# Hybrid decoder layer: later roundings of the mixer's operands, norm rows in the transposes' banks, and the tail of attention merged at its own length

## The chip, the cores and the metric

The kernel runs on one core of one Trainium2 chip. The metric is the device time of one execution in microseconds (us); lower is better. A time given for a kernel is the median of several timed runs. Besides those, one execution is taken with the hardware profiler; it has a time of its own.

## The reference, cut to what matters

A decoder layer with 1024 tokens, width 1024, batch 1, all in float32. A first SwiGLU half, then the mixer, then cross-attention to a fixed memory of 256 tokens, then a second SwiGLU half; each with an RMS norm ahead and behind. The change lies in the mixer and in the keys and values of the memory:

```python
# hybrid_mixer(u): u is the normed stream, 1024 x 1024
proj = u @ w_in
q, k, v, z, xs, bm, cm, dt_raw = jnp.split(proj, ...)
o_att = stick_breaking_attention(heads(q), heads(k), heads(v))   # 16 heads of 64
o_att = rmsnorm(o_att, attn_norm_g)
...
y = ssd_chunked(xs, dt, a, bm, cm) + d_skip[:, None] * xs
y = y.reshape(b_, s_, SSD_WIDTH) * jax.nn.silu(z)
o_ssd = rmsnorm(y in 2 groups of 512, ssd_norm_g)
return jnp.concatenate([o_att, o_ssd], axis=-1) @ w_out          # 2048 -> 1024

# stick_breaking_attention, for a block of queries t and keys s < t
z = q @ k.T / 8
log_a = log_sigmoid(z) + (sum over s < j < t of log_sigmoid(-z[t, j]))
out = exp(log_a) @ v

# memory_cross_attention
k, v = jnp.split(mem_n @ wkv, 2, axis=-1)                         # mem_n: 256 x 1024
```

## The kernel before, in words

**Products.** Every large product is made in float32 precision out of three products of rounded parts: an operand is split into a high part, rounded to the short float format that TensorE takes at full rate, and a low part, the rest. `mm3` (L139) issues high x high, high x low and low x high. A weight tile has 128 output columns and 1024 input rows (8 slices of 128, called k) and is split into `whi` (L261, ScalarE) and `wlo` (L263, VectorE). An activation operand is a tile of 128 channels x 512 tokens; where a norm's gain belongs to it, `scaled_split` makes its high part on ScalarE (L268) and its low part on VectorE (L270). The tokens are worked in two halves of 512, called hh = 0 and 1. A full weight tile with one half is 8 x 3 = 24 products.

**Order of the work.** The program is Python that issues instructions one after the other. For TensorE the order is fixed: each product is tied behind the one issued before it. Beside it runs `self.clock`, the kernel's own count of the cost of the products issued so far (0.422 per column, so 216 for a product with 512 columns, 109 for a transpose). All other engines' instructions are placed by a scheduler, which has a simulation of its own and puts an instruction into its engine's queue where it believes its inputs ready. Three means restrict it: `pinned(at)` holds a piece of work to a point of that clock; a list `self.later` holds pairs of a due time and a function, which is called when the clock has passed the due time, and its instructions are then pinned behind those issued before on their engine; and single instructions pass through `kp`, the same pin. `merge(a, ta, b, tb)` interleaves two generators of work so that they advance in the ratio ta : tb of that clock.

**The stage.** Attention goes through eight pairs of heads. While pair p computes scores, transposes and value products (`units`), the q, k and v projections of pair p + 1 (`inproj`, L1690ff) are merged with it, at 25500 : 32500. With the last pair's projections (p = 7) the function `before(n)` (L1746) is called at 13 steps, n = 0 to 12: seven of them inside the second half of the v projection, six inside the second half of the k projection. It loads the eight SSD operands of the mixer for the first half of the tokens (`XL[0][k]`, L1749, two per step for n = 0 to 3), makes their high and low parts in place (n = 5 to 12, one each), takes the first mixer weight tile (n = 5), and makes the first norm row (n = 10 and 12).

A *norm row* (`rms_rows`, L339) spreads four columns of reciprocal norms, one value per token, over all 128 partitions: four small float32 products (eight instructions in the trace) into a bank of PSUM, here of the tile "ms", then a copy on ScalarE (L349) into `rpre0` or `rpre1`. Two such rows are made for the mixer, one for each of the two SSD groups.

Scores go to PSUM in two buffers `z`, a sigmoid on ScalarE (L1780) writes them to `nb`, and a scan on VectorE (L1784) makes the attention weights in place. These are transposed on TensorE in blocks of four 128 x 128 tiles. The banks for the transposes come from `tr_tile`, a rotation of three: two buffers "tr", then "ms":

```python
turn[0] = (turn[0] + 1) % 3
if turn[0]:
    return self.t(pp, shape, F32, "tr", bufs=2)
return self.t(self.msp, shape, F32, "ms", bufs=1)
```

Each block is then split into `ath` (L261, ScalarE) and `atl` (L263, VectorE), and four value products follow once three blocks are pending. `finish` (L1797 to L1801) evacuates a result and adds it to the mixer's buffer in DRAM (`mix_d`).

**The tail.** After the last projections, `tail()` (L1902) holds the rest of pair 7's attention. `beside()` (L1907) holds the second norm row, six (MIXED) weight tiles of the mixer's SSD half (`mix_first`, L1929, four steps each), and then the values of the memory (`mem_prep`, L1861, loads and splits the memory; `memory_values`, L1872, makes eight products of 24 instructions with 256 columns). The two are merged at 26000 : 52200. `vout` transposes each memory value; the last one is pinned 2500 behind the end of the merge (L1926).

**The mixer behind it.** `mix_out` (L1958) loads the eight attention operands of the first half (`load`, L1978, DMA at L1988, kt = 0 to 7), rounds them (`scaled_split`), and has them squared: `square` (L1968) squares operand 0 into the sum `asum`, and each later one into a tile "sq1", which VectorE then adds to `asum` (L1976). The squares stand in `self.later`, at 500 + 700 kt of the clock behind the loads. The last two tiles of `mix_first` run; then the pass n = 1 takes the eight attention operands, four k of two weight tiles first and then the other four. The norm of the attention output is made from `asum` by small products (`rms_cols`) at 6600 and later. Pass 2 and 3 do the same for the other half of the tokens. The tiles "sq1" and "dg" are shared with the attention: `parts` uses both for the roundings of q and k, `mix_sum` uses "sq1" in the mixer's first tiles, and the last memory value lies in "dg".

Of the kernel before, what the change touches and what calls it, by code (L numbers as in the profile page):

```python
# [10 lines left out]
F32 = mybir.dt.float32  # L11
# [7 lines left out]
P = 128  # L19
S = 1024  # L20
H = 512
# [4 lines left out]
MIXED = 6  # L26
# [21 lines left out]
class Kern:  # L48
# [287 lines left out]
        if r2 is not None:  # L336
            self.kp(nc.vector.tensor_tensor(out=c, in0=c, in1=r2, op=ALU.mult))

    def rms_rows(self, c, r, behind=False):  # L339

        nc = self.nc
        pool, tag = self.msp, "ms"
        nb = c.shape[1]

        def product():
            ps = self.t(pool, [P, H], F32, tag, bufs=1)
            for b in range(nb):
                self.mm(ps[:, b * P : (b + 1) * P], c[:, b : b + 1].to_broadcast([P, P]), self.ident, True, True)
            self.kp(nc.scalar.copy(r, ps[:, 0 : nb * P]))  # L349

        if not behind:
            product()
        return product

# [1256 lines left out]
    def attention(self):  # L1611
        nc, ap = self.nc, self.ap
        with self.pools("at", ["o", "a"], ["w"]) as (op, sp, wsp, pp):
# [52 lines left out]
            def inproj(p):  # L1666
# [12 lines left out]
                def steps(hh, t, before):  # L1679

                    nc.sync.dma_start(out=self.mix_d[p][:, hh * H : (hh + 1) * H], in_=t)
                    dv = self.t(sp, [P, H], F32, "dv", bufs=2)
                    with first():
                        nc.vector.tensor_tensor(out=dv[:, 1:H], in0=t[:, 0 : H - 1], in1=t[:, 1:H], op=ALU.subtract)
                        if before is None:
                            nc.vector.tensor_scalar(out=dv[:, 0:1], in0=t[:, 0:1], scalar1=-1.0, scalar2=None, op0=ALU.mult)
                        else:
                            nc.vector.tensor_tensor(out=dv[:, 0:1], in0=before[:, H - 1 : H], in1=t[:, 0:1], op=ALU.subtract)
                    return dv
# [39 lines left out]
                for n in range(7):  # L1729
                    next(v1)  # L1730
                    if p == 7:
                        before(n)
                    yield
                tv.append(steps(1, evac((yield from v1), 1), t0))
                last = self.proj(wk, 1)
                for n in range(6):
                    next(last)
                    if p == 7:
                        before(7 + n)
                    yield  # L1740
                    if n in (2, 5):
                        vtr(n // 3, tv[n // 3])
                        yield
                kevac(evac((yield from last), 1), h1)

            def before(n):  # L1746

                for k in range(2 * n, 2 * n + 2) if n < 4 else ():
                    nc.sync.dma_start(out=self.XL[0][k].bitcast(F32), in_=self.mix_d[8 + k][:, 0:H])  # L1749
                if n > 4:  # L1750
                    lo = self.XL[0][n - 5]
                    self.scaled_split(self.XH[0][n - 5], lo, lo.bitcast(F32), self.par("ssd_norm_g", n - 5))
                if n == 5:
                    ready.append(next(self.Wo))
                if n == 10:
                    late.append(mix_row(0))
                if n == 12:
                    late.pop()()

            def mix_row(i):  # L1760
                self.mix_r.append(self.t(self.rp, [P, H], F32, f"rpre{i}", bufs=1))
                return self.rms_rows(self.norm_c[i][:, 0:4], self.mix_r[i], True)

            def scores(p, a, c):

# [76 lines left out]
            def drain(n):  # L1842
                while len(prods) > n:
                    prods.pop(0)[1]()
                    yield

            def values(p, a, c, A):
                for jj in range(c + 1):
                    prods.append((p, transpose(p, a, c, A, jj)))
                    yield  # L1850
                    yield from drain(3)

            def units(p):
                for a in range(2):
                    for c in range(4):
                        A = yield from scores(p, a, c)
                        if pend:
                            yield from values(*pend.pop())
                        pend.append((p, a, c, A))

            def mem_prep():  # L1861
                m = [self.t(sp, [P, 4, MEM], F32R, t, bufs=3) for t in ("q", "k", "v")]
                m = [x[:, 2 * i : 2 * i + 2, :] for x in m for i in range(2)]
                m += [x.rearrange("p (a b) -> p a b", a=2) for x in spare]
                for i in range(4):
                    raw = self.t(sp, [P, 2, MEM], F32, "ev", bufs=2)
                    nc.sync.dma_start(out=raw, in_=ap["memT"][:, 2 * i : 2 * i + 2, :])
                    for j in range(2):
                        self.scaled_split(m[i][:, j, :], m[4 + i][:, j, :], raw[:, j, :], self.par("mem_g", 2 * i + j))
                return m[0:4], m[4:8]  # L1870

            def memory_values(mh, ml):  # L1872

                rm = self.t(self.tp, [P, H], F32, "sq1")[:, 0:MEM]
                self.rms_rows(self.mem_c[:, :], rm)
                yield
                for n in range(8):
                    w = ready.pop() if ready else next(Wm)
                    ps = yield from self.kvproj(w, mh, ml)

                    t = self.t(self.tp, [P, H], F32, "dg") if n == 7 else self.t(sp, [P, H], F32, "ev", bufs=2)
                    t = t[:, 0:MEM]
                    with first():
                        nc.vector.tensor_tensor(out=t, in0=ps, in1=rm, op=ALU.mult)
                    pend_v.append((n, t))
                    if n > 0:
                        vout(*pend_v.pop(0))
                        yield
# [13 lines left out]
            def tail():  # L1902
                yield from units(7)
                yield from values(*pend.pop())
                yield from drain(0)

            def beside():  # L1907
                late.append(mix_row(1))
                self.first = self.mix_first(ready.pop())
                for n in range(4 * MIXED):  # L1910
                    if n == 2:
                        late.pop()()
                    if n == 4 * MIXED - 4:
                        ready.append(next(Wm))
                    next(self.first)
                    yield
                yield from memory_values(*mem_prep())
# [3 lines left out]
            self.Wo, self.mix_r, ready, late = self.wstream(wo[0:MIXED]), [], [], []  # L1921
            for p in range(7):
                self.merge(units(p), 25500 if p else 20700, inproj(p + 1), 32500)
            self.merge(tail(), 26000, beside(), 21000 + 5200 * MIXED)
            self.Wo = self.wstream(wo[MIXED:])
            with self.pinned(self.clock + 2500):  # L1926
                vout(*pend_v.pop(0))
# [30 lines left out]
    def mix_out(self):  # L1958
# [3 lines left out]
        with self.pools("mo", ["r", "a"], ["b"]) as (rp, sp, sp2, dnp):  # L1962
# [5 lines left out]
            def square(i, x):  # L1968

                if i == 0:  # L1970
                    asum.append(self.t(sp, [P, H], F32, "asum"))
                    nc.scalar.square(asum[-1], x)
                else:
                    sq = self.t(self.tp, [P, H], F32, "sq1")
                    nc.scalar.square(sq, x)
                    nc.vector.tensor_tensor(out=asum[-1], in0=asum[-1], in1=sq, op=ALU.add)  # L1976

            def load(kt, hh):  # L1978
                if kt < 8:
                    hi = self.t(sp, [P, H], F32R, "ohi", bufs=8)  # L1980
                    lo = self.t(sp, [P, H], F32R, "olo", bufs=8)
                else:
                    hi, lo = self.XH[1][kt % 8], self.t(sp2, [P, H], F32R, "slo", bufs=8)
                    if kt == 8:
                        self.place(sp2, 32)
                raw = self.t(sp, [P, H], F32, "oraw", bufs=8) if kt < 8 else lo.bitcast(F32)
                self.tc.keep_in_program_order(
                    nc.sync.dma_start(out=raw, in_=self.mix_d[kt][:, hh * H : (hh + 1) * H])  # L1988
                )
                if kt < 8:  # L1990
                    self.later.append((self.clock + (500, 3000)[hh] + (700, 1300)[hh] * (kt % (8, 3)[hh]), lambda: square(kt, raw)))
                self.scaled_split(hi, lo, raw, self.par("ssd_norm_g" if kt >= 8 else "attn_norm_g", kt % 8))
                return hi, lo

            passes = [(hh, part) for hh in range(2) for part in (1, 0)]
# [3 lines left out]
            def prefetch(n, k):  # L1999
                if n < 4:  # L2000
                    hh, part = passes[n]
                    acts.setdefault(n, []).append(load(8 * part + k, hh))
# [11 lines left out]
            for n, (hh, part) in enumerate(passes):  # L2014
# [13 lines left out]
                for d0 in range(0, 8, 2):  # L2028
                    ws = [next(W), next(W)]
                    ps = {}  # L2030
# [383 lines left out]
```

## Time and profile before

| what | us |
|---|---|
| median of 3 runs | 2599.42 |
| lowest and highest of these runs | 2598.77 and 2601.72 |
| the profiled execution's own time | 2599.88 |
| span of the profile (first to last instruction) | 2598.1 |
| TensorE busy in the span | 2572.6 (99%) |
| VectorE busy in the span | 1991.7 (77%) |
| ScalarE busy in the span | 1291.8 (50%) |

The profile is one execution, its times count from the start of the span. PE is TensorE's matrix products, PEld its weight loads, DVE is VectorE, ACT is ScalarE, POOL is GpSimd and SP the engine that issues most DMAs. A row of a single instruction gives its start, its duration, engine, line, operation and tiles (out<-in); in brackets stands the idle time of the engine just before it and what ended that idle time. `mm`, `dn`, `z`, `tr`, `ms` are tiles in PSUM; `L139` is the line of the helper that issues all products.

### The profile page before, as it was taken

To read this page: it belongs to the slowest core of one execution; us is meant where nothing else is said; L and a number is where in the kernel's file an instruction comes from. 1 tells how busy PE (TensorE), PEld (TensorE's weight loads), DVE (VectorE), ACT (ScalarE), POOL (GpSimd) and SP (SyncE) were. 2 spreads that over 40 slices of the span, in tenths; PEclk is the share of its full clock that TensorE was granted. 3 is DMA by queue.
4 is the path that set the end of the run, shared out by engine and by line. 5 is a ranking of instruction groups with operands and counts; after the bars stand their busy time and mean duration, and the time that the engine had idled before them with its cause. 6 is when DMAs were issued, how large, how long until landed. Compare 5 with 4: busy or idle time off the path is not lost. (4 is left out here: it accounts for less than half of the span.)

```text
span 2598.1 us, 36782 instructions
## 1 busy us (share of the span) xinstructions
PE 2572.6 (99%) x12850; PEld 2147.1 (83%) x12850; DVE 1991.7 (77%) x3045; ACT 1291.8 (50%) x2300; POOL 576.1 (22%) x668
## 2 busy tenths in 40 slices
PE   9999999999999999999999999999999999999999
PEld 7888888887777788888888898888878888888887
DVE  7889997779689884777777777876656888767767
ACT  7434444555356663555555554445554433333553
POOL 2555553001000001111111110111011755541000
PEclk9999999999999999999999999999999999999999
DMA  6448889655555526555555556647658453327554
GB/s 239 162 174 298 305 293 315 204 186 184 206 209 193 183 70 218 162 154 145 148 155 133 157 171 208 205 162 251 203 182 300 144 176 102 115 80 239 184 175 153
DMA packets 216042, 489.82 MB, mean 189 GB/s; under 512 B 26544, under 2 KB 35120, under 8 KB 215856
## 3 DMA queue, kind: packets, MB, share of 16 engines
q1 hardware_dynamic: 169232, 381.02, 44.9%
q0 software_dynamic: 22720, 62.93, 8.1%
q10 hardware_dynamic: 23904, 43.53, 4.5%
q8 instruction: 101, 1.65, 0.3%
q14 instruction: 85, 0.70, 0.1%
HBM read 327.46 MB, written 138.94 MB: 180 GB/s over the span
## 5 line engine op out<-in xcount | busy, mean ns | idle before, releaser
L139 PE MATMUL mm<-xh,whi 128*128 128x512 f32 x1312 | 519.4, 405 | 3.9 <-ACT xh L268 2.0
L139 PE MATMUL mm<-xh,wlo 128*128 128x512 f32 x1280 | 491.3, 391 | 0.0
L139 PE MATMUL mm<-xl,whi 128*128 128x512 f32 (+1 forms) x1248 | 485.2, 389 | 0.4 <-DVE xl L270 0.3
L139 PEld LDWEIGHTS mm<-xh,whi 128*128 128x128 f32 x1312 | 246.8, 188 | 45.6 <-issue 3.8
L139 PEld LDWEIGHTS mm<-xh,wlo 128*128 128x128 f32 x1280 | 240.3, 188 | 52.4 <-DVE wlo L263 0.4
L139 PEld LDWEIGHTS mm<-xl,whi 128*128 128x128 f32 x1248 | 235.4, 189 | 34.4 <-DVE xl L270 1.5
L1784 DVE TENSOR_TENSOR_SCAN nb<-nb,begin 128x128 f32<-128x128 f32 (+7 forms) x128 | 171.6, 1352 | 41.7 <-ACT nb L1780 40.1
L1780 ACT ACTIVATE nb<-z,scale 128x128 f32<-128x128 f32 (+2 forms) x192 | 108.2, 581 | 70.3 <-PE z L139 69.4
L263 DVE TENSOR_TENSOR wlo<-wraw,whi 128x1024 fp32r<-128x1024 f32 x70 | 85.5, 1221 | 51.9 <-ACT whi L261 51.6
L261 ACT CAST whi<-wraw 128x1024 fp32r<-128x1024 f32 (+1 forms) x86 | 83.5, 970 | 73.2 <-PE mm L139 50.9
L1801 POOL DMA_DIRECT2D mix<-sq x64 | 52.9, 826 | 248.2 <-DVE sq L1799 194.9
L658 ACT ACTIVATE ft<-ft 128x512 f32<-128x512 f32 x88 | 55.5, 632 | 94.7 <-DVE ft L657 94.1
L139 PE MATMUL dn<-xh,wlo 128*128 128x512 f32 x296 | 101.2, 389 | 0.0
L761 POOL TENSOR_TENSOR wc<-raw,wraw 128x512 f32<-128x512 f32 x55 | 80.7, 1467 | 55.5 <-DVE wlo L263 23.4
L263 DVE TENSOR_TENSOR atl<-tr,ath 128x512 fp32r<-128x512 f32 (+1 forms) x107 | 67.4, 631 | 32.6 <-ACT ath L261 32.1
L761 POOL TENSOR_TENSOR wc<-wraw,raw 128x512 f32<-128x512 f32 x56 | 78.7, 1405 | 52.1 <-DVE blk L263 16.7
L858 POOL TENSOR_TENSOR ft<-ft,e 128x512 f32<-128x512 f32 x37 | 59.8, 1616 | 124.4 <-DVE e L854 56.5
L261 ACT CAST ath<-tr 128x512 fp32r<-128x512 f32 (+1 forms) x107 | 58.4, 546 | 58.0 <-PE tr L142 55.5
L139 PE MATMUL dn<-xh,blk 128*128 128x512 f32 x264 | 85.2, 389 | 0.0
L139 PE MATMUL mm<-ath,v 128*128 128x256 f32 x320 | 84.6, 287 | 0.4 <-ACT sq L1798 0.3
L139 PE MATMUL mm<-atl,v 128*128 128x256 f32 x320 | 83.0, 282 | 0.7 <-DVE atl L263 0.7
L139 PE MATMUL dn<-xh,whi 128*128 128x512 f32 x240 | 82.9, 390 | 0.0
(580 smaller groups left out, 6738.1 us busy)
## 6 DMA issues: line engine op xcount, KB each, us to landing
whi<-dwhi SPq DMA_DIRECT2D x82, 512.0 KB, 3.7
wlo<-dwlo SPq DMA_DIRECT2D x82, 512.0 KB, 4.9
wraw<-in_w_gu SPq DMA_DIRECT2D x43, 512.0 KB, 4.1
dwhi<-bh SPq DMA_DIRECT2D x78, 256.0 KB, 4.1
dwlo<-bl SPq DMA_DIRECT2D x78, 256.0 KB, 4.1
raw<-in_w_gu SPq DMA_DIRECT2D x37, 512.0 KB, 4.2
wraw<-xs SPq DMA_DIRECT2D x56, 256.0 KB, 3.0
xs<-ft ACTq DMA_DIRECT2D x54, 256.0 KB, 2.8
```

What stands on the lines that cost most here:

```text
L139: self._pe(self.nc.tensor.matmul(out, lhsT, rhs, start=start, stop=stop, skip_group_check=self.more), cost)
L261: self.kp(self.nc.scalar.copy(hi, src))
L263: self.nc.vector.tensor_tensor(out=lo, in0=src, in1=hi.bitcast(F32), op=ALU.subtract)
L658: nc.scalar.activation(t, t, AF.Silu)
L761: inst = (nc.vector if early else nc.gpsimd).tensor_tensor(out=t, in0=a, in1=b, op=op)
L858: nc.gpsimd.tensor_tensor(out=t1, in0=t1, in1=e, op=ALU.mult)
L1780: nc.scalar.activation(nb[:, s0:s1], z[:, 0:n], AF.Sigmoid, scale=sc[:, i : i + 1])
L1784: nc.vector.tensor_tensor_scan(out=nb[:, 0:Wd][:, ::-1], data0=nb[:, 0:Wd][:, ::-1], data1=begin[:, S - Wd : S][:, ::-1], initial=0.0, op0 ...
L1801: nc.gpsimd.dma_start(out=self.mix_d[p][a * 64 : a * 64 + 64, csl], in_=o, accum_op=ALU.add)
```

## The change

Five edits, all within the last 180 us of attention and mixer:

1. `before(n)` rounds operand n - 8 for n > 7, where it rounded operand n - 5 for n > 4. So operands 0 to 4 are rounded at the steps 8 to 12; operands 5 and 6 come at the first step of `beside()` and operand 7 at its second. The loads stay where they are.
2. The two norm rows of the mixer take their PSUM tile from `tr_tile`, the rotation of the transposes, and not from "ms" in every case. The argument `behind` of `rms_rows` was a flag and is now the function that gives the tile.
3. The tail is merged with its 28500 in place of 26000, against the same 52200.
4. The squares of the mixer's attention operands alternate between the tiles "sq1" and "dg".
5. Attention operands 4 to 7 of the first half are rounded by way of `self.later`, at 7000 + 700 (kt - 4) of the clock behind their load; they were rounded right behind their load in the text.

```diff
-    def rms_rows(self, c, r, behind=False):
+    def rms_rows(self, c, r, behind=None):
         nc = self.nc
-        pool, tag = self.msp, "ms"
         nb = c.shape[1]

         def product():
-            ps = self.t(pool, [P, H], F32, tag, bufs=1)
+            ps = behind([P, H]) if behind else self.t(self.msp, [P, H], F32, "ms", bufs=1)
             ...
-        if not behind:
+        if behind is None:
             product()
         return product
...
             def before(n):
...
-                if n > 4:
-                    lo = self.XL[0][n - 5]
-                    self.scaled_split(self.XH[0][n - 5], lo, lo.bitcast(F32), self.par("ssd_norm_g", n - 5))
+                if n > 7:
+                    mix_split(n - 8)
...
+            def mix_split(k):
+                lo = self.XL[0][k]
+                self.scaled_split(self.XH[0][k], lo, lo.bitcast(F32), self.par("ssd_norm_g", k))
+
             def mix_row(i):
                 self.mix_r.append(self.t(self.rp, [P, H], F32, f"rpre{i}", bufs=1))
-                return self.rms_rows(self.norm_c[i][:, 0:4], self.mix_r[i], True)
+                return self.rms_rows(self.norm_c[i][:, 0:4], self.mix_r[i], tr_tile)
...
             def beside():
                 ...
                 for n in range(4 * MIXED):
+                    if n < 2:
+                        for k in ((5, 6), (7,))[n]:
+                            mix_split(k)
...
-            self.merge(tail(), 26000, beside(), 21000 + 5200 * MIXED)
+            self.merge(tail(), 28500, beside(), 21000 + 5200 * MIXED)
...
             def square(i, x):
...
-                    sq = self.t(self.tp, [P, H], F32, "sq1")
+                    sq = self.t(self.tp, [P, H], F32, ("sq1", "dg")[i % 2])
...
             def load(kt, hh):
...
-                self.scaled_split(hi, lo, raw, self.par("ssd_norm_g" if kt >= 8 else "attn_norm_g", kt % 8))
+                g = self.par("ssd_norm_g" if kt >= 8 else "attn_norm_g", kt % 8)
+                if 4 <= kt < 8 and hh == 0:
+                    self.later.append((self.clock + 7000 + 700 * (kt - 4), lambda: self.scaled_split(hi, lo, raw, g)))
+                else:
+                    self.scaled_split(hi, lo, raw, g)
                 return hi, lo
```

## The prediction

> **What bounds the kernel now.** I read the page first, then the busy time by stages around the edited code, then who TensorE waited for there, then single instructions in order of time.
>
> ```profile
> span 2598.1 us, 36782 instructions
> PE 2572.6 (99%) x12850; PEld 2147.1 (83%) x12850; DVE 1991.7 (77%) x3045; ACT 1291.8 (50%) x2300; POOL 576.1 (22%) x668
> ```
>
> TensorE (PE) is busy in 99% of the span, and the change takes no matrix product away. So only the moments in which TensorE stands still can be won: 25.5 us in all.
>
> ```profile
> 1420.00:1459.00 39.00, 36.59 (x218) 31.48 (x216) 32.32 (x49) 24.63 (x51) 6.17 (x16) 1.00 0.56 164
> 1459.00:1546.60 87.60, 87.26 (x581) 79.47 (x580) 67.34 (x96) 46.16 (x89) 9.94 (x25) 1.00 0.52 155
> 1546.60:1550.40 3.80, 2.98 (x24) 2.58 (x22) 3.19 (x6) 2.14 (x5) 1.17 (x3) 1.00 0.69 233
> 1550.40:1561.50 11.10, 11.10 (x52) 9.16 (x51) 6.14 (x10) 6.93 (x13) 0.82 (x1) 1.00 1.01 327
> 1561.50:1576.00 14.50, 13.35 (x63) 10.55 (x62) 13.40 (x20) 10.46 (x16) 0.00 (x0) 1.00 0.62 215
> 1576.00:2598.00 1022.00, 1013.07 (x4681) 841.90 (x4679) 748.46 (x1159) 452.23 (x798) 249.82 (x254) 1.00 0.54 179
> ```
>
> The columns are the stretch, its length, then busy time and instructions of PE, its weight loads, VectorE (DVE), ScalarE (ACT) and GpSimd, then the granted clock. The edited code runs from 1420 to 1576: projections of the last head pair (to 1459), that pair's attention beside mixer and memory products (to 1550.4), then the mixer. TensorE's idle time there is 2.41 + 0.34 + 0.82 + 0.00 + 1.15 = 4.7 us. The waits of those 160 us name its owners (total, times, longest):
>
> ```profile
> PE mm L139 <- ACT sq L1798: 1.7, 2, 1.4
> PE mm L139 <- DVE atl L263: 0.7, 1, 0.7
> PE ms L142 <- ACT rpre L349: 0.7, 1, 0.7
> PE ms L139 <- DVE asum L1976: 0.7, 1, 0.7
> PE dn L139 <- DVE wlo L263: 0.5, 1, 0.5
> PE z L139 <- ACT nb L1780: 0.3, 1, 0.3
> ```
>
> These idle times count from the modelled end of the product before, and products overlap:
>
> ```profile
> 1550.40 0.40 PE L139 MATMUL mm<-xh,whi 128*128 128x512 f32 x1
> 1550.63 0.40 PE L139 MATMUL mm<-xl,whi 128*128 128x512 f32 x1
> ```
>
> A product lasts 0.40 and the next starts after 0.23, so a stop costs its idle time plus about 0.16 us. That is the unit used below.
>
> **The change part by part.** *Mixer operands rounded three steps later.* The eight roundings of the SSD operands (L268 on ACT, L270 on DVE) move from steps 5 to 12 of the last projections to steps 8 to 12 and the first two steps of the mixer. They are as many and as long, no DMA moves with them, and they pass nothing on SP's or POOL's queue. What they could win is the longest stop:
>
> ```profile
> 1432.21 0.72 ACT L268 ACTIVATE xh<-xl,params 128x512 fp32r<-128x512 f32 x1 [3.06 <-DMA xl<-mix]
> 1432.85 0.57 ACT L261 CAST ath<-tr 128x512 fp32r<-128x512 f32 x1
> 1434.87 0.50 PE L139 MATMUL mm<-xh,whi 128*128 128x512 f32 x1 [1.41 <-ACT sq L1798]
> 1435.94 0.68 DVE L1676 TENSOR_TENSOR ev<-mm,rpre 128x512 f32<-128x512 f32 x1
> 1466.84 0.91 ACT L268 ACTIVATE q<-ev,params 128x256 fp32r<-128x256 f32 x2 [0.83 <-DMA ev<-in_memT]
> 1509.42 0.61 PE L139 MATMUL ms<-ident,cmem 128*128 128x128 f32 x4
> ```
>
> ACT stood 3.06 us behind a rounding whose load had not landed; the attention's cast and evacuation stood behind it, and TensorE lost 1.41 + 0.16 = 1.57. But look where that rounding ran: at 1432.21, when the v projection's first half was not yet evacuated (1435.94). In the text it belongs some six steps into the second half, which comes after that. The order on ACT is therefore not the text's: a planner puts an instruction where it believes its data ready. The memory tiles show how far this goes: their rounding runs at 1466.84, while the text places it behind the mixer's 24 steps, just ahead of the product of 1509.42: 43 us early. These roundings carry no pin to the text's order, their data are ready when they were, and everything between the old and the new place in the text becomes ready later than they do. So I take 0 for this part. If the order did follow, the gain is 1.57, and 0.3 + 0.16 for the wait of z on ACT, also amid these roundings: 2.0. The other end is a rounding of operands 5 to 7 that comes too late for the third step: one ACT and one DVE instruction of 0.7, a loss of 1.4 at most. [...]
>
> *Norm rows in the transposes' banks.* The eight products of each norm row leave the fixed bank "ms" for the next in the rotation of two "tr" buffers and "ms".
>
> ```profile
> 1449.12 0.60 PE L142 MATMUL tr<-ident,dv 128*128 128x128 f32 x4
> 1453.01 1.05 PE L139 MATMUL ms<-ident,cy 128*128 128x128 f32 x8
> 1453.95 0.39 DVE L263 TENSOR_TENSOR v<-tr,v 128x256 fp32r<-128x256 f32 x1
> 1454.10 0.59 ACT L349 COPY rpre<-ms 128x512 f32<-128x512 f32 x1 [0.59 <-PE ms L139]
> 1454.26 0.67 DVE L263 TENSOR_TENSOR atl<-tr,ath 128x512 fp32r<-128x512 f32 x1
> 1454.73 0.66 PE L142 MATMUL ms<-ident,nb 128*128 128x128 f32 x4 [0.68 <-ACT rpre L349]
> ```
>
> Today the turn after the first row is "ms", so the transposes wait for the row's copy (to 1454.69) and lose 0.68 + 0.16 = 0.84. Afterwards the row itself takes "ms", which was its turn, and the transposes take the "tr" buffer filled at 1449.12. Its last reader, kept back by other DVE work, ends at 1453.95 + 0.39 = 1454.34. The start moves from 1454.73 to about 1454.4: a gain of 0.3, which I take. The bounds are 0.84, and a loss of 0.2 if it is the other buffer (read until 1454.93). The second row stops nothing today. It shifts the rotation of the later banks, and with it the two small stops between 1459 and 1546 (0.34 idle): 0 taken, 0.7 either way.
>
> *Tail merged by its length.* In the kernel's own costs the tail is 28265: 8414 of score products, 16488 of transposes and value products, 3363 left by pair 6. The work beside it is 54677: six mixer tiles of 24 products at 216 (31113), rows 1296, eight memory products of 2593, seven small transposes of 218. At 26000 to 52200 the side work ends when the tail has done 54677 x 26000 / 52200 = 27234, and some 1030, rounded up to whole steps, runs alone:
>
> ```profile
> 1546.61 0.38 PE L142 MATMUL tr<-ident,ev 128*128 128x128 f32 x2
> 1547.29 1.23 DVE L263 TENSOR_TENSOR wlo<-wraw,whi 128x1024 fp32r<-128x1024 f32 x1
> 1548.46 0.28 PE L139 MATMUL mm<-atl,v 128*128 128x256 f32 x1
> 1548.87 0.38 PE L139 MATMUL mm<-ath,v 128*128 128x256 f32 x1
> 1549.94 0.39 PE L139 MATMUL mm<-atl,v 128*128 128x256 f32 x1 [0.69 <-DVE atl L263]
> ```
>
> After 1546.61 only attention is left; its last operand waits on DVE behind a weight's 1.23 us. The steps of 0.41 and 1.07 should be 0.12: 1.24 lost. At 28500 the tail ends when the side work has done 28265 x 52200 / 28500 = 51770, and what runs alone is the last memory product (2593) with its small transposes, whose operands were rounded long before. That loses nothing, and the weight split of 1547.29 moves behind it, since it needs the buffer that the product reads. Taken: 1.24. Bounds: 1.24 and, as attention now has less filler per step (0.546 of its work per unit of side work, before 0.498), 0.8 lost, about the 0.82 idle of that stretch.
>
> *Half of the attention roundings later, squares in two tiles.* Operands 4 to 7 are rounded at 7000 to 9100 of the planner's clock, now with a pin behind the squares, and the squares alternate between two tiles. The mixer's DVE and ACT work, by rows:
>
> ```profile
> L270 DVE SCALAR_TENSOR_TENSOR olo<-oraw,params,ohi 128x512 fp32r<-128x512 f32 x8 | 5.7, 747 | 2.4 <-ACT ohi L268 2.4
> L1976 DVE TENSOR_TENSOR asum<-asum,sq 128x512 f32<-128x512 f32 x3 | 2.1, 685 | 0.0
> 1555.68 0.72 ACT L268 ACTIVATE ohi<-oraw,params 128x512 fp32r<-128x512 f32 x1 [1.73 <-DMA oraw<-mix]
> 1564.10 1.22 DVE L263 TENSOR_TENSOR wlo<-wraw,whi 128x1024 fp32r<-128x1024 f32 x1
> 1565.38 0.50 PE L139 MATMUL dn<-ohi,wlo 128*128 128x512 f32 x1 [0.48 <-DVE wlo L263]
> 1573.48 0.68 DVE L1976 TENSOR_TENSOR asum<-asum,sq 128x512 f32<-128x512 f32 x1
> 1574.32 1.02 PE L139 MATMUL ms<-small,asum 128*128 128x1 f32 x8 [0.67 <-DVE asum L1976]
> ```
>
> DVE works without a pause until 1565.3 and makes the second weight tile last: 0.48 + 0.16 = 0.64 lost. The sum of squares ends at 1574.2, and its column sums stop TensorE for 0.67 + 0.16 = 0.83. With the pin all squares come ahead of operand 4, so the sum is done some 10 us earlier: 0.83 won (bounds 0 and 0.83). Ahead of the second weight tile DVE then has four roundings and seven sums, 3.0 + 4.8 = 7.8, against eight roundings and three sums, 5.7 + 2.1 = 7.8: the same work. But the first operand loads need no longer wait for the very end (V of the last pair is released with the tail, some 3 us ahead of the merge's end), so it starts earlier: 0.64 won. The other end is the rival below. Operand 4 is needed 24 products after the pass begins at 1561.5, at 1567.0, and its rounding, by order behind the squares, is ready near 1565; that is the cover, 2 us.
>
> **Sum.** 0 + 0.3 + 1.24 + 0.64 + 0.83 = 3.0 us. The profiled execution took 2599.9, 1.8 more than its span, and gives 2596.9; the median of the runs shown (2599.42) lies 0.5 below it, so 2596.4.
>
> **Rivals.** *The roundings do move* (0.22): the pair of 3.06 and 1432.85 rows dissolves, 2.0 more, 2594.4, and 2593.9 if the norm row also wins its 0.84. For it: the loads do land by 1437. Against it: the 43 us.
>
> *The stops only change their names* (0.18): ACT and DVE are 77% and 50% loaded over the span, and between 1561.5 and 1576 DVE is busy 13.40 of 14.50, so what is taken from one wait is found in the next. Half of the sum goes: 2598.
>
> *Slower: the second weight tile behind the squares* (0.10). Its split is not pinned; the pinned squares, sums and operands 4 to 7 stand earlier in the text. If they all get ahead on DVE, its queue holds eight roundings (5.7), seven sums (4.8) and three sums of the mixer's last tiles (2.1): 12.6 from 1556.4, so the tile is split at 1569.0 + 1.2 = 1570.2 and not at 1565.3, 4.9 more. Less the other terms (0.3 + 1.24 + 0.83) that is 2.5 slower: 2601.9. It decides once that split ends over 2.4 us later, after 1567.7 on the old clock. Against it: the tile is ready for ACT near 1559, and both engines pause between pinned sums. [...]
>
> **How the numbers follow.** The forecast has 0.50, and 2596.4 is its time. A measurement of this kernel can tell about 0.2% (5 us) from no change. Forecast and second rival lie inside that but for a tail (0.06 faster), the first rival half outside (0.14), the third mostly inside (0.05 slower). So faster 0.20, same 0.75, slower 0.05. The range goes from 2593.2 (every gain at its bound, 6.2 with the rotation's 0.7) to 2600.6 (half way from no change into the slower one); all losses at their bounds (1.4, 0.2, 0.7, 0.8, 4.9) would make 2607.4, which needs all of them at once and is left out.
>
> **What would show it.** Right: an xh rounding on ACT still waits about 3 us for its load near 1432, with the 1.4 us stop of TensorE behind it; no wait of transposes on the row's copy over 0.4; the merge ends on a memory product without a stop; no wait on asum; the second weight tile ends ahead of its product. Wrong: that first stop is gone (first rival), or the wait on wlo grows past 2.4 us (third). A stop that grows behind 1600, where 1013.07 of 1022 us are busy, would be none of my steps.

## The result

The changed kernel takes 2602.14 us (median of 22 runs, 2599.35 to 2604.53) against 2599.04 (22 runs): the ratio is 1.0014, with an interval of 1.0008 to 1.0020. It is a little slower, where 2596.4 was forecast. The first lines of the profile's page after it:

```profile
span 2597.6 us, 36805 instructions
PE 2572.1 (99%) x12850; PEld 2147.8 (83%) x12850; DVE 1991.4 (77%) x3045; ACT 1291.5 (50%) x2300; POOL 575.4 (22%) x668
```

The page alone misleads. Its execution took 2599.35, the fastest of the 22, so its span is below that of before. What can be compared is the stretch that the change touches, between the same two products in both traces (before, then after):

```profile
1396.59 0.39 PE L139 MATMUL mm<-xl,whi 128*128 128x512 f32 x1
...
1561.57 0.39 PE L139 MATMUL dn<-ohi,whi 128*128 128x512 f32 x1
...
1648.85 0.39 PE L139 MATMUL dn<-slo,whi 128*128 128x512 f32 x1
```

```profile
1394.70 0.40 PE L139 MATMUL mm<-xl,whi 128*128 128x512 f32 x1
...
1557.16 0.39 PE L139 MATMUL dn<-ohi,whi 128*128 128x512 f32 x1
...
1649.80 0.39 PE L139 MATMUL dn<-slo,whi 128*128 128x512 f32 x1
```

Before it lasts 252.26 us, after 255.10: 2.84 more, and the medians differ by 3.10. The middle row of each is the first product with an attention operand. Up to there the changed kernel needs 162.46 in place of 164.98, so it gains 2.5; from there on 92.64 in place of 87.28, so it loses 5.4. The last of the prediction's edited stages, at the same times of the new trace, shows where (stretch, length, busy time and instructions of PE, weight loads, DVE, ACT and POOL, then the granted clock, the share of the DMA engines and GB/s):

```profile
1561.50:1576.00 14.50, 10.57 (x43) 8.17 (x42) 12.88 (x20) 9.85 (x16) 0.00 (x0) 0.88 0.46 164
```

PE runs 43 products there where it ran 63, and the granted clock is 0.88. What TensorE waits for between 1420 and 1580 (total, times, longest):

```profile
PE dn L139 <- DVE olo L270: 2.3, 3, 1.8
PE dn L139 <- ACT ohi L268: 2.1, 1, 2.1
PE mm L139 <- ACT sq L1800: 1.1, 1, 1.1
PE tr L142 <- DVE v L263: 0.4, 1, 0.4
PE z L139 <- ACT nb L1782: 0.4, 1, 0.4
```

The waits on `wlo`, on `asum`, on `rpre` and on the tail's `atl` are gone. In their place stand waits on the attention operands, `ohi` and `olo`. Instruction by instruction, the engines mixed in order of time:

```profile
1558.69 0.71 ACT L268 ACTIVATE ohi<-oraw,params 128x512 fp32r<-128x512 f32 x1
...
1562.75 0.63 ACT L1980 ACTIVATE dg<-oraw 128x512 f32<-128x512 f32 x1 [0.84 <-DVE asum L1981]
...
1563.48 0.39 PE L139 MATMUL dn<-ohi,wlo 128*128 128x512 f32 x1
...
1564.70 0.61 ACT L1980 ACTIVATE dg<-oraw 128x512 f32<-128x512 f32 x1
...
1565.22 2.54 ACT L268 ACTIVATE ohi<-oraw,params 128x512 fp32r<-128x512 f32 x4
...
1565.98 0.49 PE L139 MATMUL dn<-ohi,whi 128*128 128x512 f32 x1 [2.11 <-ACT ohi L268]
...
1567.49 2.73 DVE L270 SCALAR_TENSOR_TENSOR olo<-oraw,params,ohi 128x512 fp32r<-128x512 f32 x4
...
1568.29 0.79 PE L139 MATMUL dn<-olo,whi 128*128 128x512 f32 x1 [1.81 <-DVE olo L270]
```

ScalarE rounds operand 3 at 1558.69 and operand 4 only at 1565.22, behind the last square. TensorE wants operand 4 right behind 1563.48, stands 2.27 us for its high part and 2.08 for its low part (start to start, less the usual 0.23), and the product at 1568.29 lasts 0.79 in place of 0.39. The clock by stretches (length, PE busy and products, granted clock, DMA share and GB/s):

```profile
1564.53:1567.94 3.41, 0.49 (x1) 1.00 0.92 333
1567.94:1571.35 3.41, 3.06 (x7) 0.50 0.09 32
1571.35:1574.77 3.42, 3.42 (x19) 1.00 0.00 0
```

For 3.41 us the clock is halved. TensorE works for 3.06 of them, so this costs about 1.5; the rest lies inside the stop. With two stops of 0.4 at operands 1 and 3 the bill of the mixer's beginning is 4.35 + 0.8 + 1.5 = 6.7, less the waits won on `wlo` and `asum` (0.64 + 0.83): 5.2 of the 5.4.

### The profile page after: what moved, and what is told of

Same layout as the page of the kernel before. It is cut to its first block, busy times and chain, and to the rows that moved or that the text cites. A ratio compares the mean times of both kernels' runs of the same rounds, so it can differ in the third digit from the quotient of the medians.

```text
span 2597.6 us, 36805 instructions
## 1 busy us (share of the span) xinstructions
PE 2572.1 (99%) x12850; PEld 2147.8 (83%) x12850; DVE 1991.4 (77%) x3045; ACT 1291.5 (50%) x2300; POOL 575.4 (22%) x668
## 4 chain that ended last, share of the span: by engine, by line
PE 76%; issue 13%; DVE 4%; DMA 2%; ACT 1%; POOL 0%; SPq 0%; DVEq 0%; ACTq 0%; POOLq 0%
PE mm L139 38%; PE dn L139 32%; PE z L139 2%; PE tr L142 2%; PE ms L142 1%; PE ms L139 1%; DMA wraw<-xs 0%; DVE hl L263 0%; DVE nb L1786 0%; DVE wlo L263 0%; DVE F L404 0%; DMA xl<-mix 0%; DMA oraw<-mix 0%; PE mm L142 0%; DVE xl L416 0%
## 5 line engine op out<-in xcount | busy, mean ns | idle before, releaser
L261 ACT CAST wlo<-wc 128x512 fp32r<-128x512 f32 x79 | 49.1, 621 | 68.0 <-PE dn L139 23.2
```

The lines of the kernel that those rows point to most:

```text
L261: self.kp(self.nc.scalar.copy(hi, src))
```

## The experiments

Theory A: the deferral (edit 5) put operands 4 to 7 behind all seven squares on both engines, and the stop there, with the halved clock behind it, is the loss; the other four edits gain. Rival B: TensorE comes too early for loads that land when they always did. Rival C: the halved clock falls at random. "Stretch" below is the time between the two products of the last section, worked out in each trace; before it is 252.26.

**Edit 5 undone, edit 5 alone, edits 1 to 3 alone, edit 5 with an earlier due time.**

```diff
 # undo_operands: the changed kernel with
-                if 4 <= kt < 8 and hh == 0:
-                    self.later.append((self.clock + 7000 + 700 * (kt - 4), lambda: self.scaled_split(hi, lo, raw, g)))
-                else:
-                    self.scaled_split(hi, lo, raw, g)
+                self.scaled_split(hi, lo, raw, g)
 # only_operands: these lines, the other way round, in the kernel before
 # undo_operands_squares: undo_operands with
-                    sq = self.t(self.tp, [P, H], F32, ("sq1", "dg")[i % 2])
+                    sq = self.t(self.tp, [P, H], F32, "sq1")
 # operands_between: the changed kernel with
-                    self.later.append((self.clock + 7000 + 700 * (kt - 4), ...
+                    self.later.append((self.clock + 400 + 700 * kt, ...
```

> The changed kernel with one edit undone: attention operands 4 to 7 of the first half are rounded right behind their load in the text, as before; the other four edits stay. Theory A (the deferred roundings stand on ScalarE and VectorE behind all seven squares, and TensorE waits for operand 4): the stops of 2.27 and 2.08 us at 1563 to 1568 go, and with them the 3.41 us at half clock behind them (1.7 us). The time falls by 5 to 6 us from the changed kernel's 2602.1, to 2596 to 2597, below the kernel before (2599.0). Rival B (TensorE merely comes too early for loads that land when they always did): the stop stays about as long and only changes its name, 2600 to 2602. Rival C (the loss is a half-clock period that falls at random, not the stop): the same 2602 within 1.

> The kernel before with this one edit alone: operands 4 to 7 rounded by way of the list of later work, behind the squares, which still share one tile. Theory A: operand 4 is ready only behind the seventh square, near 1568 to 1573, and TensorE, which wants it at 1567.0, stops for 2 to 6 us; with a half-clock period 1.7 more: 2601 to 2606. Rival B: TensorE comes no earlier than before, so the 2 us of cover hold: 2599, within 0.5. Rival C: 2599.

> The first three edits alone (later roundings of the SSD operands, norm rows in the rotation, tail at 28500); one tile for the squares, operands 4 to 7 as before. Theory A: the 2.4 us that TensorE gained ahead of the mixer stay in the end, and the wait of the column sums on the sum of squares (0.8) is back: 2596.5 to 2597.5. Rival B: the operands' loads land as late as before, so the 2.4 us are given back as stops at operands 0 to 3: 2599.

> The changed kernel with the deferral kept but due earlier: operand kt at 400 + 700 kt of the clock behind its load, which puts each of the four just ahead of its own square in place of behind all of them. Theory A, place in the queue decides and not the pin as such: operand 4 is ready some 3 us earlier, the stop at it is at most 1.5 us, and no half-clock period follows: 2597 to 2599. If the pin itself is what costs, 2601 to 2602.

The kernel before took 2598.68 beside these four. undo_operands took 2596.30 (ratio 0.9991, 0.9983 to 1.0000), so the interval just reaches no change; its stretch is 249.88, 2.4 less than before. Its ScalarE row of the roundings and what TensorE waited for from 1550 to 1580:

```profile
1558.38 1.93 ACT L268 ACTIVATE ohi<-oraw,params 128x512 fp32r<-128x512 f32 x3
```

```profile
PE ms L139 <- DVE asum L1981: 0.7, 1, 0.7
PE dn L139 <- DVE olo L270: 0.2, 1, 0.2
```

Operands 3 to 5 are rounded in one go, the stops at operand 4 and the halved clock are gone: theory A. Of B a stop of 0.41 start to start is left. The wait for the sum of squares is back, so in the changed kernel it was edit 5 that had removed it, not the two tiles.

only_operands took 2605.54 (1.0025, 1.0016 to 1.0034), stretch 257.55: more than the changed kernel loses, as neither B nor C allows. The roundings come behind squares that share one tile, each waiting for VectorE; the last one waits for the tile itself, which a sum of the mixer holds:

```profile
1568.02 0.63 ACT L1975 ACTIVATE sq<-oraw 128x512 f32<-128x512 f32 x1 [1.29 <-DVE asum L1976]
...
1570.91 0.63 ACT L1975 ACTIVATE sq<-oraw 128x512 f32<-128x512 f32 x1 [2.26 <-DVE xl L1956]
...
1571.44 1.93 ACT L268 ACTIVATE ohi<-oraw,params 128x512 fp32r<-128x512 f32 x3
...
1572.20 0.79 PE L139 MATMUL dn<-ohi,whi 128*128 128x512 f32 x1 [5.45 <-ACT ohi L268]
```

So the two tiles of edit 4 had softened the loss of edit 5: 5.61 us of stop here, 4.35 there. Two periods at half clock, 6.8 us in all, begin inside this stop, at 1569.52.

undo_operands_squares took 2597.06 (0.9996, 0.9987 to 1.0005), stretch 250.77. The time is as expected, but the wait of the column sums on the sum of squares does not come; TensorE stands 1.10 for another sum of the mixer (`sq`, L1960) near 1584. operands_between 2597.01 (0.9994, 0.9985 to 1.0002), stretch 250.70. In the latter the deferral and its pin stay, only the place in the queue is earlier, and the stops at operands 4 to 7 shrink to two of 0.46: the place decides, not the pin. Each of these two is not clearly faster than before by its interval; by its stretch it gains 1.5.

**The tail and the squares.** undo_tail is the changed kernel with 26000; only_tail and tail_squares are the kernel before with 28500, the second with two tiles for the squares as well.

```diff
-            self.merge(tail(), 26000, beside(), 21000 + 5200 * MIXED)
+            self.merge(tail(), 28500, beside(), 21000 + 5200 * MIXED)
```

> The kernel before with the tail merged at 28500 in place of 26000 and nothing else. Theory A: the steps of 0.29 and 0.95 us in which attention ran alone (1.24) go, TensorE comes to the mixer 1.2 us earlier, and since the operands' roundings have 5 us of cover in the old order, the gain stays: 2597 to 2598, against 2598.7 of the kernel before on this chip. Rival: the second weight tile, late by 0.64 already, is now late by 1.8, and the time is 2598.7.

> The changed kernel with the tail merged at 26000 again; the other four edits stay. Theory A (operand 4 stands behind seven squares, wherever TensorE is): the stop of 1.24 us at the end of attention is back, TensorE comes to operand 4 some 1.5 us later than in the changed kernel, and the two stops there shrink by about as much, to 2.5 to 3.5 us in sum: 2600.5 to 2602.5. Rival (the cover of 2 us was right for the old arrival, and only TensorE's earlier arrival spent it): no stop over 0.6 at operand 4, 2597 to 2599.

> The kernel before with the tail at 28500 and the squares in two tiles, operands 4 to 7 in their old place. Theory A (with one tile each square waits for VectorE to add the one before, and the sum's end sets when TensorE may go on, so with the tail alone the 1.24 us came back as a longer wait for the sum, 2.5 us, and a half-clock period): the wait for the sum is under 1 us and no half-clock period follows: 2596.5 to 2598. Rival (the sum is late because its loads are): the wait stays above 2 us, 2599.5 to 2600.5.

only_tail took 2600.09 against 2598.82 (1.0004, 0.9995 to 1.0013), stretch 254.18. That missed the expectation. The stop of 1.24 at the tail's end is gone and TensorE is 2.0 us earlier at its first operand. But it now stands 2.48 at the sum of squares: counted from the start of the stretch it comes there 2.8 earlier than before, the sum only 1.2. The clock is halved for two periods:

```profile
1570.83 0.39 PE L139 MATMUL dn<-ohi,whi 128*128 128x512 f32 x1
1573.54 1.84 PE L139 MATMUL ms<-small,asum 128*128 128x1 f32 x8 [2.32 <-DVE asum L1976]
1575.24 0.77 PE L139 MATMUL dn<-olo,whi 128*128 128x512 f32 x1
```

tail_squares took 2596.88 against 2599.56 (0.9991, 0.9982 to 1.0000), stretch 251.05: with the second tile no wait for the sum is left, though stops of 1.35 and 0.69 at the second weight tile are. undo_tail took 2600.32 against 2599.56 (1.0003, 0.9994 to 1.0012), stretch 254.35. The stop at operand 4 is 2.45, where theory A had 2.5 to 3.5 and the rival at most 0.6. The time is just under theory A's range, and only because of a stop that nobody had named; without its 1.83 the time would lie in the rival's range, so it is the stop at operand 4 that tells the two apart:

```profile
1507.41 0.49 PE L142 MATMUL ms<-ident,nb 128*128 128x128 f32 x3
1509.57 0.60 PE L139 MATMUL ms<-ident,cmem 128*128 128x128 f32 x3 [1.67 <-DVE atl L263]
...
1569.92 0.50 PE L139 MATMUL dn<-olo,whi 128*128 128x512 f32 x1 [2.29 <-DVE olo L270]
```

The first two rows are edit 2 in a bad place, as far as they show. With the rotation shifted by the norm rows, a transpose takes "ms" just ahead of the memory's own norm row, which still has "ms" for its fixed bank, and 1.83 us are lost until the transposes are read. In the changed kernel the merge at 28500 happens to avoid it.

**Roundings tied to their place, and a kernel that beats both.** roundings_pinned is undo_operands with the SSD roundings tied behind the instruction issued before them; ahead_pinned has this and edit 5 with operand kt ahead of square kt - 1; ahead_pinned_store has the last memory value stored by GpSimd besides.

```diff
             def mix_split(k):
                 lo = self.XL[0][k]
+                self.inlater, held = True, self.inlater
                 self.scaled_split(self.XH[0][k], lo, ...)
+                self.inlater = held
 # ahead_pinned
-                    self.later.append((self.clock + 7000 + 700 * (kt - 4), ...
+                    self.later.append((self.clock + 400 + 700 * (kt - 1), ...
 # ahead_pinned_store
-                nc.sync.dma_start(out=self.kv_d[n // 2][1]...
+                (nc.sync if n < 7 else nc.gpsimd).dma_start(out=self.kv_d[n // 2][1]...
```

> The changed kernel with operands 4 to 7 as before, and the eight SSD roundings tied to their place in the program's text. Theory A (the move in the text did nothing because the scheduler put them back at the very same places; tied, they let the attention's casts pass): the 1.4 us stop near 1431 goes, nothing else grows over 0.4: 2594.5 to 2595.5. Rival (the stops only change their names, ScalarE being busy with scores later on): a new stop of 1 us or more between 1440 and 1480, and 2596 to 2597.

> The changed kernel with the SSD roundings tied as in the run before, and operand kt of 4 to 7 due at 400 + 700 (kt - 1), so ahead of square kt - 1: one square earlier than where two stops of 0.46 us were left. Theory A: no stop over 0.3 at operands 4 to 7 and none of the column sums (0.8 where they are not tied): 2594 to 2595. Rival (ScalarE and VectorE are full there, what comes earlier pushes something else out): stops of 0.8 to 1.3 us remain in the pass under other names: 2595 to 2596.

> The kernel of the run before, with the store of the last memory value issued by GpSimd, so that SP's queue no longer holds the operands' loads behind it. Theory A (the loads start where that store lets them): the first operand is rounded about 1 us earlier and the two stops of 0.4 us at operands 1 to 3 go: 0.5 to 0.9 us less than the run before. Rival (the loads wait for the tiles of attention or for the memory's bandwidth): the first rounding stays where it is, same time within 0.5.

The kernel before took 2598.82 beside them. roundings_pinned took 2595.32 (0.9986, 0.9977 to 0.9995), stretch 248.86. The first rounding on ScalarE is now at 1445.29 and waits for nothing:

```profile
1445.29 0.71 ACT L268 ACTIVATE xh<-xl,params 128x512 fp32r<-128x512 f32 x1
```

The stop near 1431 (1.42 in undo_operands) is gone; the one behind the first norm row grew from 0.60 to 1.05, so that 1.0 of the stretch is left as the gain. ahead_pinned took 2594.15 (0.9983, 0.9974 to 0.9992), stretch 248.52; ahead_pinned_store 2594.10 (0.9981, 0.9973 to 0.9990), stretch 247.28. Its store gives the loads their way: in ahead_pinned they stand in SP's queue behind the `kv` stores, in ahead_pinned_store behind one only (SP's rows of the two, in this order):

```profile
1550.02 1.86 SPq L1904 DMA_DIRECT2D kv<-vo  x2
1552.10 4.49 SPq L1995 DMA_DIRECT2D oraw<-mix  x8
```

```profile
1549.74 0.52 SPq L1904 DMA_DIRECT2D kv<-vo  x1
1550.49 4.87 SPq L1995 DMA_DIRECT2D oraw<-mix  x8
```

No stop over 0.2 is left at the beginning of that kernel's mixer; the first rounding starts 1.3 earlier in the stretch, as theory A had it. In the stretch the store is worth 1.2; the medians, where 0.5 to 0.9 was expected, differ by 0.05 and do not show it. Against the kernel before the whole is 4.7 us.

## Why the prediction was wrong

The measured 2602.14 lies above the range's end of 2600.6. Slower by 0.12 to 0.14% is inside the 0.2% that the prediction itself called no change, which had 0.75; but the sign of the forecast was wrong. Point by point:

- *SSD roundings, 0*: right, and for the reason given. The changed kernel's ScalarE still runs them at the old places, with the wait for the load still there:

```profile
1429.58 0.72 ACT L268 ACTIVATE xh<-xl,params 128x512 fp32r<-128x512 f32 x1 [2.31 <-DMA xl<-mix]
...
1432.65 0.50 PE L139 MATMUL mm<-xh,whi 128*128 128x512 f32 x1 [1.09 <-ACT sq L1800]
```

  The stop is 1.25 there, 1.57 before, and 1.25 to 1.81 in the other untied kernels whether they have the edit or not, so that difference is not the edit's. Tied, the move removes the stop, as the first rival said, and wins 1.0.
- *Norm row, 0.3*: right; 0.84 became 0.60. The bound on the shifted rotation, 0.7, was too small: undo_tail shows 1.83.
- *Tail, 1.24*: the stop went, as worked out. That attention would lack filler showed as a stop of 0.60 at 1473 (only_tail has it too), inside the bound of 0.8, while three of 0.48, 0.42 and 0.25 went. With the 0.32 at 1431 these are most of why 2.5 were won ahead of the mixer, not 1.5; the prediction had put 0 on them.
- *Second weight tile, 0.64, and sum of squares, 0.83*: both waits went, the second for the reason given. The first went for another reason than that the loads start earlier. The first issues of the loads on SP's queue, before and after:

```profile
1550.59 2.98 SPq L1988 DMA_DIRECT2D oraw<-mix  x5
1550.76 4.26 SPq L1993 DMA_DIRECT2D oraw<-mix  x8
```

  Counted from the start of the stretch (1396.59 and 1394.70) that is 154.0 before and 156.1 after: 2 us later, all eight behind the last stores of the memory. In only_tail the first is issued at 151.1, so there the reasoning held; with edits 1 to 3 (undo_operands_squares) it is at 156.1 again, and which of edits 1 and 2 undoes it no run tells. The second weight tile's split is simply done at 1552.78 instead of 1564.10, ahead of the operands on both engines.
- *The step that failed* is the cover of operand 4: "its rounding, by order behind the squares, is ready near 1565", needed at 1567.0. In place of 2 us ahead of the need, its low part came 4.4 behind it (the stops of 2.27 and 2.08). Counted from the start of the stretch, the need was forecast at 170.4 and came at 169.0: 2.5 were won ahead of the mixer, and 0.8 given back at operands 1 and 3. So the terms could not be added without taking them from this cover. The larger error is the readiness, forecast at 168.4 and measured at 173.5 (1567.49 and one rounding of 0.7, in the trace's own time). Of these 5.1, 1.5 are the later loads: VectorE begins its first low part at 161.3, and the sum had taken over the 159.9 of before. The rest is work that the sum did not have. It held four roundings and seven sums, 7.8. From the first low part to operand 4's VectorE takes 11.5 (1556.01 to 1567.49) and is busy for 10.89 of them. Besides those eleven it makes the split of a weight tile, three sums of the mixer's tiles (the first of them, L1957, at 1556.67) and a low part `slo` at 1565.02, which are 3.7 from start to start:

```profile
1560.89 1.23 DVE L263 TENSOR_TENSOR wlo<-wraw,whi 128x1024 fp32r<-128x1024 f32 x1
...
1565.69 0.68 DVE L1960 TENSOR_TENSOR sq<-mm,rpre 128x512 f32<-128x512 f32 x1
1566.29 0.68 DVE L1981 TENSOR_TENSOR asum<-asum,dg 128x512 f32<-128x512 f32 x1
1566.89 0.68 DVE L1961 TENSOR_TENSOR xl<-xl,sq 128x512 f32<-128x512 f32 x1
```

  ScalarE inherits this: the square at 1562.75 waited 0.84 for an addition (at 1562.04) that stood behind that weight split. undo_tail shows that the readiness alone was enough to lose the cover: there TensorE wants operand 4's low part at 171.8 of the stretch, later than the forecast need, and still stands 2.45.
- *The slower rival* gave 2601.9 and named its cause in kind, a queue behind pinned squares, but not the victim: the weight tile was never late, operands 4 to 7 were, and its deciding point (a split 2.4 later) was not reached. The order that it supposed on DVE, with that split behind the squares, the changed kernel does not show: there the split was done at 1552.78, ahead of the operands. That the figure fits is chance; it knew nothing of the halved clock, 1.5 of the loss.
- *The stops only change their names* is what happened to the tail alone: only_tail gives all of it back at the sum. (The text has the loads of the two engines the wrong way round: it is DVE that is busy 77% of the span and ACT 50%.)

## What to carry to other kernels

Work that is deferred and pinned inherits the queue in front of it (here operand 4 was rounded at 1565.22, behind the last square, and its low part came 4.4 us after the need): add up all that stands there on each engine, the work that is not part of the chain too, and the handovers where two engines share one tile. Gains ahead of a handover shorten every cover behind it, so subtract them from the cover before adding them to the sum. Compare times of two traces from a common instruction, not from the start of the span. And an edit in the program's text moves nothing where a scheduler places the instruction; see first that the order on the engine changes.

## What was not expected of the hardware

In the changed kernel the loss at operand 4 was more than its stops: beside their 4.35 us the clock was halved for 3.41 us, which cost about 1.5 more. Inside the work the halved clock lasts 3.41 us in before and in the changed kernel, and 6.8 in only_operands and only_tail; undo_operands and tail_squares, whose profiled runs have a granted clock of 1.0, show none. In the two traces of before and of the changed kernel its beginnings lie whole multiples of 3.4133 apart (before: 649.04 and, behind the last product, 2594.64, which are 570 periods; the changed kernel: 1567.94 and 2595.35, which are 301). Stretch, length, PE busy and products, clock, DMA share and GB/s for two periods each of before, of undo_tail at two places (the second counted on from the halved period of the first) and of only_tail:

```profile
645.63:649.04 3.41, 1.74 (x5) 1.00 1.01 398
649.04:652.45 3.41, 3.41 (x9) 0.50 1.03 404
```

```profile
644.56:647.97 3.41, 1.90 (x8) 1.00 0.90 328
647.97:651.38 3.41, 3.32 (x8) 0.50 1.03 401
...
1566.16:1569.57 3.41, 1.47 (x7) 1.00 0.52 169
1569.57:1572.98 3.41, 3.06 (x13) 1.00 0.86 297
```

```profile
1569.86:1573.27 3.41, 1.36 (x7) 1.00 0.42 153
1573.27:1576.69 3.42, 3.15 (x12) 0.50 0.47 156
```

What decides is not shown. It is not the busy time of the period ahead alone: 1.36, 1.74 and 1.90 us are followed by half clock, 1.47 in the same trace as the 1.90 are not. (Busy time counts a lone product at its full 0.4, though in a row they follow each other every 0.23.) Nor is it the longest stop: in before TensorE sat idle for 0.89, 0.52 and 0.42 in the period ahead of 649.04, never longer, while 2.45 us of stop cost nothing more in undo_tail and 2.48 brought two periods in only_tail. Nor do the edits decide alone: before has such a period at 649 in its profile, the changed kernel, whose program is the same there, has none. Of the changed kernel's 22 runs the eleven with a granted clock of 0.999 average 2601.2, the ten with 0.998 average 2602.8. Why only_tail's second period stayed at half clock with twelve products in the one ahead stays open.
